# One decoder layer on one core: x loaded twice for its sums of squares, the final scale of a token from three sums per block, and new pacing numbers

## The chip, the cores and the metric

The kernel runs on one core of a Trainium2 chip. The metric is device time in microseconds for the whole program. A core has a matrix engine (TensorE, PE in the profile; its weight loads are PEld), a vector engine (VectorE, DVE), a scalar engine (ScalarE, ACT), a general engine (GpSimd, POOL) and a queue that issues transfers (SyncE, SP). Each runs its own instructions in order and waits on semaphores that others raise.

## The reference

One layer works on 512 tokens of width 2048 in float32. Its input is normed, multiplied by `w_in` and split between an RG-LRU branch and eight pairs of RWKV-7 heads; the two outputs go through `w_o` into the residual. A convolutional GLU follows, then a gated embedding of the token, and a last norm:

```python
u = rmsnorm(h, ln_mix[i]); z = u @ w_cat
...
h = h + jnp.concatenate([out_a, out_b], axis=-1) @ w_o[i]
u = rmsnorm(h, ln_ffn[i])
gate = causal_dwconv(u @ w_gate[i], conv_f_w[i], conv_f_b[i])
h = h + (jax.nn.gelu(gate) * (u @ w_up[i])) @ w_down[i]
u = rmsnorm(h, ln_ple[i])
e = jax.nn.sigmoid(u @ w_ple_gate[i]) * (p[i] @ w_ple_proj[i])
h = h + rmsnorm(e, ln_ple_post[i])
return rmsnorm(h, ln_final)
```

Here `rmsnorm(x, g)` is x * rsqrt(mean(x*x) + eps) * g over the features of a token.

## The kernel before, in words

**Precision.** Nearly every large product is made of three matmuls on values split into a high and a low part (`xh`, `xl` of the activations; `whi`, `wlo` of the weights): high by high, high by low, low by high. ACT makes the high part (`whi`, L123; `xh`, L139), DVE the low part (`wlo`, L124; `xl`, L140). A weight unit is a tile of 128x1024; `wfill` and `wnext` load it on SP into one of two `wraw` buffers, split it, and hand it out.

**Stages.** The *head* (0 to about 60 us) multiplies the 16 tiles of x by the 288 LoRA columns (`lora_z`, L532 to L534: 12 matmuls of 288 columns for an x tile), then begins the RWKV inputs `kt`, `rt`, `vt` of the first head pair (`rwkv_z`, 48 matmuls each). The norm's token scale is applied behind the product, so it is needed only when `kt` is finished. The sum of squares of x runs over partitions: ACT squares an x tile (`square_x`, L508), GpSimd adds it to `lt` (L509, fifteen times), and `tok_rstd` (L182) sums `lt` over partitions with four matmuls of one column. `lora_fin` is called with the number of the dense matmul of `kt`: after the tenth it transposes the LoRA outputs `vk`, `bk`, `kk` (L554, twelve transposes), at the nineteenth it calls `tok_rstd` and `derive`, at the 33rd `rstd_bcast` (L195) spreads the scale over the partitions into `rs`, which `shift` multiplies in.

*Phase 1* (to 867 us) is the token mixing. For each of eight head pairs, `prep` makes the operands, `batch` inverts a triangular matrix per chunk (`Tm`, `Tt`, `Gm`: the products L777 alternate with DVE steps L787, L805), and `chain` walks the state over eight chunks (`us` L858, `st` L879). Between their small matmuls stand dense ones: `w_in`, the LRU gates (L974 to L978) and `w_o`. `merge` writes PE's order from a table of numbers `W`, which says how much time, counted in PE time, is to pass between two steps of a part. The offsets `offp`, `offs`, `offd`, `offl`, `offt` in `W` are priorities: they set in which order the steps of `prep`, of `chain` and `batch`, of the dense products and of the LRU are put on DVE, ACT, GpSimd and SP; `offw` is that of the weight splits. The LRU step of `lru_y` has a scan on DVE (L994) whose input GpSimd makes (L993). At the end of phase 1 a new pool of PSUM tiles begins, and its first users wait for the last readers of the old one.

The *FFN* (to about 2413 us) and its turn to features follow. The *last stage* has four blocks `cb` of 512 output columns, the last of which is done in two halves of 256: per block it makes the projection `pp`, then a gate product `pg` for each of four token tiles `tt`, then `gated` (tanh, L1352), `embed` (DVE L1357 makes e, ACT L1359 sums its squares) and `post` (GpSimd multiplies by the post gain, L1363). The last section, whose order is written out by hand for PE, DVE, ACT and GpSimd, takes the last 256 columns tile by tile: 48 matmuls, tanh, e, the token's scale `rstd` (two small DVE steps L1369, L1370 and a pow on GpSimd L1371), then for the tile before it `residual` (DVE L1377 adds, ACT L1378 squares the finished residual) and `final` (multiply by scale and final gain, L1384, L1385 on ACT and GpSimd or L1387 on DVE, then the DMA out). Tiles named `tmp` have two buffers.

## Time and profile before

| what | value |
|---|---|
| device time, median of 3 runs | 2677.84 us (2676.76 to 2678.28) |
| the profiled execution's own time | 2678.29 us |
| its span in the profile | 2676.5 us |
| mean granted clock of TensorE | 0.994 |
| POOL busy | 282.5 us |
| PE busy from 2600 to 2652.2 us | 52.17 us |
| last PE instruction starts | 2651.89 us |

A row of the timeline gives the start in us, the busy time in us, the engine, the line, the operation, the tile written and the tiles read, the shape, how many instructions are merged, and in brackets the idle time ahead of it and who ended it. Busy times of following matmuls overlap, so their pace is read from the starts. The granted clock is 1.00 when TensorE runs at full speed.

### The profile page before, as it was taken

Reading aid. Unit: us, or ns where it says so; the run is one execution under the profiler, and the core shown is the slowest. Engines: PE = TensorE matmul, PEld = TensorE weight load, DVE = VectorE, ACT = ScalarE, POOL = GpSimd, SP = SyncE. Lnnn points to the kernel's source line nnn. Section 1 sums busy time; section 2 is a strip of 40 time slices with the busy share of each in tenths; the row PEclk is TensorE's granted clock in tenths of the full one; section 3 lists DMA queues with packets and bytes.
Section 4 is the critical chain, followed back from the end, with each engine's and each line's share of the span. In section 5 each row is a group of like instructions: output and inputs, shape, how many; then the busy total and the mean of one; then the engine's idle time right before and its main releaser. Section 6 shows DMA issues by size and latency. Waiting matters only on the chain.

```text
span 2676.5 us, 43392 instructions
## 1 busy us (share of the span) xinstructions
PE 2637.3 (99%) x18440; PEld 2169.2 (81%) x18440; DVE 1682.4 (63%) x2254; ACT 1081.9 (40%) x1520; POOL 282.5 (11%) x219
## 2 busy tenths in 40 slices
PE   9999999999999999999999999999999999999996
PEld 7887787787787888888888888888888888888886
DVE  7664765567564635667666766766666667775235
ACT  5563555547432433333333333333333333334344
POOL 4010100101121300000000000000000000000013
PEclk9999999999999999999999999999999999999998
DMA  5322222222342422332332323223232232332222
GB/s 172 95 76 65 85 76 67 65 84 77 103 134 76 147 87 89 108 100 98 102 103 102 102 95 102 97 100 109 97 110 96 101 107 99 99 110 87 95 88 101
DMA packets 82178, 261.35 MB, mean 98 GB/s; under 512 B 9536, under 2 KB 12224, under 8 KB 81984
## 3 DMA queue, kind: packets, MB, share of 16 engines
q1 hardware_dynamic: 81984, 258.58, 29.3%
q8 instruction: 144, 2.36, 0.4%
q14 instruction: 50, 0.41, 0.1%
...
## 4 chain that ended last, share of the span: by engine, by line
PE 72%; DVE 1%; ACT 0%; POOL 0%; issue 0%; DVEq 0%; POOLq 0%
PE wk L1178 12%; PE wk L1177 12%; PE wk L1176 12%; PE mm L1259 6%; PE mm L1260 6%; PE mm L1258 6%; PE mm L157 2%; PE mm L153 2%; PE mm L155 2%; PE mm L1345 2%; PE mm L1346 2%; PE mm L1347 2%; PE mm L1176 1%; PE mm L1177 1%; PE mm L1178 1%; DVE e L1377 0%
## 5 line engine op out<-in xcount | busy, mean ns | idle before, releaser
L123 ACT ACTIVATE whi<-wraw 128x1024 fp32r<-128x1024 f32 (+2 forms) x363 | 375.3, 1034 | 729.9 <-PE mm L155 173.5
L124 DVE TENSOR_TENSOR wlo<-wraw,whi 128x1024 fp32r<-128x1024 f32 (+2 forms) x363 | 440.6, 1214 | 238.9 <-ACT whi L123 232.9
L1176 PE MATMUL wk<-uh,whi 128*128 128x512 f32 x1408 | 547.8, 389 | 0.0
L1177 PE MATMUL wk<-ul,whi 128*128 128x512 f32 x1408 | 547.7, 389 | 0.0
L1178 PE MATMUL wk<-uh,wlo 128*128 128x512 f32 x1408 | 547.7, 389 | 0.0
L123 ACT ACTIVATE whi<-hw 128x1024 fp32r<-128x1024 f32 x154 | 163.3, 1060 | 464.2 <-PE wk L1177 418.5
L155 PE MATMUL mm<-xl,whi 128*128 128x512 f32 x832 | 332.0, 399 | 1.1 <-DVE xl L140 1.1
L153 PE MATMUL mm<-xh,whi 128*128 128x512 f32 x832 | 330.6, 398 | 1.6 <-DVE y L897 1.6
L157 PE MATMUL mm<-xh,wlo 128*128 128x512 f32 x832 | 330.8, 398 | 0.0
L1177 PEld LDWEIGHTS wk<-ul,whi 128*128 128x128 f32 x1408 | 264.3, 188 | 54.9
L1178 PEld LDWEIGHTS wk<-uh,wlo 128*128 128x128 f32 x1408 | 264.3, 188 | 54.9
L1176 PEld LDWEIGHTS wk<-uh,whi 128*128 128x128 f32 x1408 | 264.3, 188 | 54.8
L124 DVE TENSOR_TENSOR wlo<-hw,whi 128x1024 fp32r<-128x1024 f32 x154 | 188.7, 1225 | 180.8 <-ACT whi L123 178.4
L1259 PE MATMUL mm<-wlo,hid 128*128 128x512 f32 x680 | 265.1, 390 | 0.0
L1258 PE MATMUL mm<-whi,hid 128*128 128x512 f32 x680 | 264.9, 389 | 0.0
L1260 PE MATMUL mm<-whi,hid 128*128 128x512 f32 x680 | 264.8, 389 | 0.0
L1204 POOL TENSOR_TENSOR tmp<-tmp,rsa 128x512 f32<-128x512 f32 x48 | 87.6, 1825 | 1360.8 <-ACT tmp L1203 1360.8
L153 PEld LDWEIGHTS mm<-xh,whi 128*128 128x128 f32 x832 | 156.5, 188 | 36.9 <-issue 5.2
L155 PEld LDWEIGHTS mm<-xl,whi 128*128 128x128 f32 x832 | 156.6, 188 | 36.2 <-issue 2.1
L157 PEld LDWEIGHTS mm<-xh,wlo 128*128 128x128 f32 x832 | 156.5, 188 | 33.5 <-issue 1.9
L1273 DVE TENSOR_TENSOR h<-h,mm 128x512 f32<-128x512 f32 x264 | 175.2, 682 | 0.6
L1258 PEld LDWEIGHTS mm<-whi,hid 128*128 128x128 f32 x680 | 127.6, 188 | 26.4
...
## 6 DMA issues: line engine op xcount, KB each, us to landing
wraw<-wgu SPq DMA_DIRECT2D x192, 512.0 KB, 3.2
...
wraw<-wo SPq DMA_DIRECT2D x20, 256.0 KB, 2.9
tmp<-xT SPq DMA_DIRECT2D x16, 256.0 KB, 2.8
...
```

What stands on the lines that cost most here:

```text
L123: nc.scalar.activation(hi, raw, AF.Copy)
L124: nc.vector.tensor_tensor(lo, raw, hi.bitcast(F32), ALU.subtract)
L153: nc.tensor.matmul(ps, hi[:, k, :], xh, start=first and i == 0, stop=False)
L155: nc.tensor.matmul(ps, hi[:, k, :], xl, start=False, stop=False)
L157: nc.tensor.matmul(ps, lo[:, k, :], xh, start=False, stop=last and i == n - 1)
L1176: TE.matmul(ps, wh[:, k, :], xh, start=h + k == 0, stop=False)
L1177: TE.matmul(ps, wh[:, k, :], xl, start=False, stop=False)
L1178: TE.matmul(ps, wl[:, k, :], xh, start=False, stop=h == 1 and k == 7)
L1258: TE.matmul(ps, x[0][:, k, ts_], w[0][:, k, :], start=first and k == 0, stop=False)
L1259: TE.matmul(ps, x[0][:, k, ts_], w[1][:, k, :], start=False, stop=False)
L1260: TE.matmul(ps, x[1][:, k, ts_], w[0][:, k, :], start=False, stop=last and k == 1)
L1273: V.tensor_tensor(o, o, ps[tt], op)
```

## The change

In the head, x is loaded a second time, by rows of tokens (`xn`, 16 loads of 256 KB into the staging tiles that held `xT`, on SP between the weight loads). ACT squares such a tile and sums along the row in one instruction (`accum_out`, into `ssx`); one reduce, one scaling and a pow give the scale. GpSimd's adds and the four matmuls of `tok_rstd` are gone there. The transposes of the LoRA outputs come after the sixteenth dense matmul of `kt` and use a `ch` tile; the scale is made at the 41st and spread at the 31st of `rt`, and the shift of `kt` follows then. `derive` is cut in two. SP's order in the head is now written by hand with ACT's and DVE's; two more weight tiles of the LoRA are staged and the first two `wz` units are loaded right behind the constants. A third, shorter dummy matmul stands at the start.

In the last stage GpSimd keeps only the pow of single columns. With e' = e * gpost the sum of squares of a token's finished residual is made from three sums: of h*h, of e'*e' (`sg2`, ACT) and of 2*h*e' (`sb`, a DVE multiplication that also sums); `rfin` joins them with the token's scale. So e and h are multiplied by the final gain ahead (`post`, `gain`), `joined` adds them, and `final` only scales (ACT, or DVE for the last block of the last tile).

```diff
@@ the table
-W = dict(... offl=-100, offt=0, pace=790, dpace=1844, late=19660, offs=19710, offd=3000, start=1496, ... rsk=12832, ... t0=5997, tg=1544, tt=1464, lx=4608, lu=1487, ls=1435, ... per=[2, 3, 2, 2, 2, 2, 3, 0], dec7=2111)
+W = dict(... offl=100, offt=-100, pace=381, dpace=1914, late=16634, offs=3000, offd=300, start=1346, ... rsk=8216, ... t0=7550, tg=2186, tt=1559, lx=3928, lu=1429, ls=891, ... per=[2, 3, 2, 2, 3, 1, 3, 0], dec7=2070)
@@ phase1, loads
+        TE.matmul(pz[:, 0:160], z0[:, 0:128], z0[:, 0:160], start=True, stop=True)
...
+        wst = [("gt", 2), ("gt", 2), ("bv", 2), ("bv", 2), ("AR", 2), ("AR", 2), ("MQ", 2), ("NQ", 2), ("MQ", 2), ("NQ", 2)]
...
+        nc.sync.dma_start(self.con1, A["consts"][:, CKEEP:])
+        for i in range(2):
+            wload()
+        self.xn = []
@@ square_x
-            nc.scalar.activation(sq, self.xr[k], AF.Square)
-            nc.gpsimd.tensor_tensor(self.acc, self.acc, sq, ALU.add)
+    def load_xn(self, k):
+        self.xn.append(self.t(self.k1, self.stg[k], bufs=1))
+        self.nc.sync.dma_start(self.xn[k], self.A["xn"][k])
...
+        self.nc.scalar.activation(sq, self.xn[k], AF.Square, accum_out=self.ssx[:, k:k + 1])
@@ lora_z
-        with self.tc.manual_schedule(engines={ET.Activation, ET.DVE}):
+        with self.tc.manual_schedule(engines={ET.Activation, ET.DVE, ET.SP}):
+            self.loads()
...
-                    if k % 4 < 3:
-                        self.square_x(k)
+                    self.load_xn(k)
+                    for _ in range(SQX.get(k, 0)):
...
@@ lora_fin
-        if i == 9:
-            self.zp = [self.mm(), self.aux(), self.t(self.pm, "y", (128, 512), bufs=1)]
+        if i == 15:
+            self.zp = [self.t(self.pm, "ch", (128, 512), bufs=2), self.aux(), self.t(self.pm, "y", (128, 512), bufs=1)]
...
-        if i == 18:
-            self.rl = self.tok_rstd(self.acc, D, RMS_EPS, k1)
+        if i == 40:
+            m = self.pcs[:, NP - 1, 0:4]
+            nc.vector.tensor_reduce(m.unsqueeze(2), self.ssx.rearrange("p (t c) -> p t c", c=4), mybir.AxisListType.X, ALU.add)
+            nc.vector.tensor_scalar(m, m, 1.0 / D, RMS_EPS, ALU.mult, ALU.add)
+            nc.gpsimd.tensor_tensor(m, m, self.mhalf[:, 0:4], ALU.pow)
...
-        if i != 32:
+        if i == 48 + 46:
+            self.derive_lru()
+        if i == 48 + 30:
+            self.rstd_bcast(None, D, RMS_EPS, k1, self.rs, self.rl)
+        if i != 48 + 31:
@@ last stage
-        def post(tt, cb, cs=slice(0, 512)):
-            ee = e[tt * 4 + cb][:, cs]
-            G.tensor_tensor(ee, ee, gpost[cb][:, cs], ALU.mult)
+        def post(tt, cb, cs):
+            n, ix = tt * 4 + cb, slice(tt * 5 + cb, tt * 5 + cb + 1)
+            ee, j1, j2 = e[n][:, cs], T("tmp", 2)[:, cs], T("tmp", 2)[:, cs]
+            V.tensor_tensor(ee, ee, gpost[cb][:, cs], MU)
+            SC.activation(j1, ee, AF.Square, accum_out=sg2[:, ix])
+            V.scalar_tensor_tensor(j2, h3[n][:, cs], 2.0, ee, MU, MU, accum_out=sb[:, ix])
+            V.tensor_tensor(ee, ee, gfin[cb][:, cs], MU)
+        def gain(tt, cb):
+            V.tensor_tensor(h3[tt * 4 + cb], h3[tt * 4 + cb], gfin[cb], MU)
...
+        def rfin(tt, r):
+            t, at, o = T("tl", 6, (128, 1)), slice(tt, tt + 1), slice(tt * 5 + 4, tt * 5 + 5)
+            V.scalar_tensor_tensor(t, sg2[:, o], sge[:, at], r, AD, MU)
+            V.scalar_tensor_tensor(t, sb[:, o], sbe[:, at], t, AD, AD)
+            V.scalar_tensor_tensor(t, t, r, ssh[:, at], MU, AD)
+            V.tensor_scalar(t, t, 1.0 / D, RMS_EPS, MU, ALU.max)
+            return power(t)
...
-                V.scalar_tensor_tensor(e[ix], e[ix], r, h3[ix], ALU.mult, ALU.add)
-                SC.activation(h3[ix], e[ix], AF.Square, accum_out=s2[:, ix:ix + 1])
+                V.scalar_tensor_tensor(e[ix], e[ix], r, h3[ix], MU, AD)
...
-                if cb == 0 or cb == 1 and tt < 3:
-                    SC.activation(e[ix], e[ix], AF.Copy, scale=r)
-                    G.tensor_tensor(e[ix], e[ix], gfin[cb], ALU.mult)
-                else:
-                    V.scalar_tensor_tensor(e[ix], e[ix], r, gfin[cb], ALU.mult, ALU.mult)
+            if act:
+                SC.activation(e[ix], e[ix], AF.Copy, scale=r)
+            else:
+                V.tensor_scalar(e[ix], e[ix], r, None, MU)
```

How the order moves is shown at three places; in such a row stand the line, the operation, the tile written with its number, the tiles read, and the shape.

ACT at the end of the LoRA product, before: the squares (L508) stand ahead of the copies of the LoRA outputs (L540) out of PSUM.

```order
L508 ACTIVATE tmp_100_491<-ktl_152 128x512
L508 ACTIVATE tmp_105_527<-lxl_11_118 128x512
L508 ACTIVATE tmp_106_530<-kt_130 128x512
L123 ACTIVATE whi_542<-wraw_540 128x1024
L508 ACTIVATE tmp_107_533<-ta_142 128x512
L508 ACTIVATE tmp_108_536<-y_29_154 128x512
L540 ACTIVATE vk_519<-wk_176 128x288
L616 ACTIVATE lhi_867<-lraw_862 128x384
L540 ACTIVATE bk_521<-wk_177 128x288
L540 ACTIVATE kk_103_523<-ch_178 128x288
L123 ACTIVATE whi_548<-wraw_546 128x1024
L540 ACTIVATE vk_525<-ch_179 128x288
```

ACT at the same place, after: L525 is the square with its sum, L560 the copy.

```order
L143 ACTIVATE xh_102_483<-y_33_172,par 128x512
L127 ACTIVATE whi_557<-wraw_181 128x1024
L525 ACTIVATE tmp_105_489,pcs<-lx_44_199 128x512
L525 ACTIVATE tmp_106_491,pcs<-lx_49_221 128x512
L560 ACTIVATE vk_532<-wk_115 128x288
L560 ACTIVATE bk_534<-wk_116 128x288
L560 ACTIVATE kk_116_536<-ch_117 128x288
L560 ACTIVATE vk_538<-ch_118 128x288
L525 ACTIVATE tmp_107_493,pcs<-lxh_54_243 128x512
L525 ACTIVATE tmp_108_495,pcs<-lxl_59_265 128x512
L127 ACTIVATE whi_563<-wraw_561 128x1024
L525 ACTIVATE tmp_110_511,pcs<-lxh_64_287 128x512
```

Two squares stand ahead of the first copy now, none between the copies, and nothing that they write is read by GpSimd.

DVE in the batch of the seventh head pair, before: the LRU's last steps (L990 and the scan L994, which the order lists under the same operation name as other three-operand instructions; L995 behind them) beside the batch's second `Gm` (L787), its `Tm` and `Tt` (L805, L806) and the chain's `us` and `st`.

```order
L806 STREAM_TRANSPOSE Tt_7521<-Tm_7520 128x256
L990 SCALAR_TENSOR_TENSOR lxl_1031_7413<-lrc_7542,lxl_1031_7413 128x512
L858 TENSOR_TENSOR us_7746<-ch_7743,NQ_6465 128x64
L994 SCALAR_TENSOR_TENSOR lxl_1029_7404<-lrc_7542,lxl_1031_7413 128x512
L787 TENSOR_TENSOR Gm_7788<-wk_7755,con_157 128x8x16
L995 TENSOR_TENSOR lxl_1029_7404<-lxl_1029_7404,row_172 128x512
L879 SCALAR_TENSOR_TENSOR st_7808<-ch_7748,pcs,so_7809 128x64
L805 TENSOR_TENSOR Tm_7520<-wk_7814,Tm_7520 128x32x4
L806 STREAM_TRANSPOSE Tt_7521<-Tm_7520 128x256
```

DVE in the same batch, after, at its first `Gm` (L822; L805 is the transposition that finishes `Tm`, L452 and L455 a shift, L893 `us`, L1025, L1029 and L1030 the LRU's steps, L128 a weight split):

```order
L804 TENSOR_TENSOR Tt_7625<-Tt_7625,Tm_7624 128x256
L805 STREAM_TRANSPOSE Tm_7624<-Tt_7625 128x256
L452 TENSOR_TENSOR zs<-mm_7535,rs_94 128x512
L1025 SCALAR_TENSOR_TENSOR lxl_1035_7393<-lrc_7500,lxl_1035_7393 128x512
L128 TENSOR_TENSOR wlo_7656<-wraw_7653,whi_7655 128x1024
L455 SCALAR_TENSOR_TENSOR kt_7647<-zs,par,tmp_1082_7649 128x512
L1029 SCALAR_TENSOR_TENSOR lxl_1031_7375<-lrc_7500,lxl_1035_7393 128x512
L1030 TENSOR_TENSOR lxl_1031_7375<-lxl_1031_7375,row_111 128x512
L893 TENSOR_TENSOR us_7680<-ch_7677,NQ_6539 128x64
L822 TENSOR_TENSOR Gm_7722<-wk_7689,con_175 128x8x16
L771 TENSOR_TENSOR NQ_7603<-wk_7724,con_175 128x512
```

The scan stood one row ahead of the second `Gm` and two rows behind L990; now it stands three rows ahead of the first `Gm`, with a split and the end of a shift between it and L1025.

DVE in the last section, before: one whole slot, from the tile's e (L1357) to the four residual additions (L1377).

```order
L1357 SCALAR_TENSOR_TENSOR e_21331<-tmp_22744,hw_3458_22260 128x256
L1369 TENSOR_REDUCE tl_22750<-s_21319 128x1
L1370 TENSOR_SCALAR tl_22750<-tl_22750 128x1
L1369 TENSOR_REDUCE tl_22754<-ss 128x1
L1370 TENSOR_SCALAR tl_22754<-tl_22754 128x1
L1387 SCALAR_TENSOR_TENSOR e_21326<-e_21326,tl_22750,hw_3326_21298 128x512
L1387 SCALAR_TENSOR_TENSOR e_21327<-e_21327,tl_22750,hw_3326_21298 128x512
L1377 SCALAR_TENSOR_TENSOR e_21328<-e_21328,tl_22754,h_8_10608 128x512
L1377 SCALAR_TENSOR_TENSOR e_21329<-e_21329,tl_22754,h_9_10609 128x512
L1377 SCALAR_TENSOR_TENSOR e_21330<-e_21330,tl_22754,h_10_10610 128x512
L1377 SCALAR_TENSOR_TENSOR e_21331<-e_21331,tl_22754,h_11_10611 128x512
```

DVE in the last section, after: the slot of the last tile, from its tanh's first reader (L1507) on; L1444 is `joined`, L1430 and L1435 to L1438 are single columns.

```order
L1507 SCALAR_TENSOR_TENSOR tmp_22961<-tmp_22960,hw_3497_22348 128x256
L1511 SCALAR_TENSOR_TENSOR e_21351<-tmp_22960,hw_3497_22348 128x256
L1444 SCALAR_TENSOR_TENSOR e_21346<-e_21346,tl_22891,h_10_10619 128x512
L1430 TENSOR_SCALAR tl_22970<-ss,se 128x1
L1516 SCALAR_TENSOR_TENSOR tmp_22961,sb<-qz_21328,e_21351 128x256
L1517 TENSOR_TENSOR e_21351<-e_21351,hw_3339_21307 128x256
L1444 SCALAR_TENSOR_TENSOR e_21347<-e_21347,tl_22891,h_11_10620 128x512
L1435 SCALAR_TENSOR_TENSOR tl_22981<-sg_21330,sge,tl_22972 128x1
L1436 SCALAR_TENSOR_TENSOR tl_22981<-sb,sbe,tl_22981 128x1
L1437 SCALAR_TENSOR_TENSOR tl_22981<-tl_22981,tl_22972,ssh 128x1
L1438 TENSOR_SCALAR tl_22981<-tl_22981 128x1
L1444 SCALAR_TENSOR_TENSOR e_21348<-e_21348,tl_22972,h_12_10621 128x512
```

Two multiplications by scale and gain (L1387) and two reduces have left DVE's slot; three operations of 256 columns and four single columns have come in, and the four additions stand between them.

More of the change, by code (lines that the diff above doesn't have):

```diff
@@ L79, in shape_constants @@
     return c
+SQX = {14: 4, 15: 4}
 class Builder:
@@ L253, in phase1, with loads @@
             TE.matmul(pz, z0[:, 0:128], z0, start=True, stop=True)
-        stg = ["lx0", "lx1", "lxh0", "lxl0", "lxh1", "lxl1", "lrc", "kt", "rt", "vt", "Sq", "ta", "kk", "bt", "ktl", "y1"]
-        wst = [("gt", 2), ("gt", 2), ("bv", 2), ("bv", 2), ("AR", 2), ("AR", 2), ("MQ", 2), ("NQ", 2)]
+        TE.matmul(pz[:, 0:160], z0[:, 0:128], z0[:, 0:160], start=True, stop=True)
+        self.scadd = cp.tile([128, NC, C + 1], F32, name="scadd")
+        G.memset(self.scadd, 0.0)
+        G.memset(self.scadd[:, :, 0:1], 1.0)
+        self.TT = cp.tile([128, NC, C], F32, name="TT")
+        G.memset(self.TT, 0.0)
+        self.llo = cp.tile([128, 3, 128], F32R, name="llo")
+        G.memset(self.llo.bitcast(F32), 0.0)
+        self.pcs = cp.tile([128, NP, NC], F32, name="pcs")
+        self.ssx = self.pcs[:, NP - 3:NP - 1].rearrange("p a c -> p (a c)")
+        self.zs = cp.tile([128, S + 1], F32, name="zs")
+        G.memset(self.zs[:, 0:1], 0.0)
+        self.zc = self.t(self.cp, "row", (128, S + 3), bufs=1)
+        G.memset(self.zc[:, 0:3], 0.0)
+        self.zdone = {}
+        self.prepped = {}
+        self.batched = {}
+        with self.tc.manual_schedule(engines={mybir.EngineType.PE}):
+            self.merge(self.dense_stream(self.order))
+    def loads(self):
+        nc, A, k1 = self.nc, self.A, self.k1
+        stg = self.stg = ["lx0", "lx1", "lxh0", "lxl0", "lxh1", "lxl1", "lrc", "kt", "rt", "vt", "Sq", "ta", "kk", "bt", "ktl", "y1"]
+        wst = [("gt", 2), ("gt", 2), ("bv", 2), ("bv", 2), ("AR", 2), ("AR", 2), ("MQ", 2), ("NQ", 2), ("MQ", 2), ("NQ", 2)]
         self.xr, self.wraw = [], []
@@ L541, in lora_z @@
             self.zl.append(z)
-        for k in range(3, KT, 4):
+        for k in range(nsq, KT):
             self.square_x(k)
@@ L591, in rwkv_z, with fin @@
             ps = self.mm()
+            def fin(ps, n, m_, o_):
+                d[n] = self.t(k1, n, bufs=1)
+                self.shift(ps, self.P(m_, j), self.dv(o_, j), d[n])
             for i, _ in enumerate(self.dense(ps, 2, self.xs)):
-                if j == 0 and n == "kt":
-                    self.lora_fin(i)
+                if j == 0 and n != "vt":
+                    self.lora_fin(i if n == "kt" else 48 + i)
+                    if n == "rt" and i == 30:
+                        fin(*first)
                 yield
-            d[n] = self.t(k1, n, bufs=1)
-            self.shift(ps, self.P(m_, j), self.dv(o_, j), d[n])
+            if j == 0 and n == "kt":
+                first = ps, n, m_, o_
+            else:
+                fin(ps, n, m_, o_)
         self.zdone[j] = (d["kt"], d["rt"], d["vt"])
@@ L1332, in phase2 @@
         rsh = k2.tile([128, 4], F32, name="rsh")
+        hq = [T("q" + n, 1, (128, 2, 512)) for n in "xz"]
         ss = k2.tile([128, 20], F32, name="ss")
-        s2 = k2.tile([128, 16], F32, name="s2")
+        sg2, sb = (k2.tile([128, 20], F32, name=n) for n in ("sg2", "sb"))
+        se, sge, sbe, ssh = (k2.tile([128, 4], F32, name=n) for n in ("se", "sge", "sbe", "ssh"))
+        MU, AD = ALU.mult, ALU.add
         e = [self.bp.tile([128, S], F32, tag="x%s%d" % ("hl"[i // 8], 8 + i % 8), name="e%d" % i, bufs=1) for i in range(16)]
@@ new lines, in phase2, with power, early @@
+        AX = mybir.AxisListType.X
+        five = lambda t, tt: t[:, tt * 5:tt * 5 + 5]
+        def power(m):
+            r = T("tl", 6, (128, 1))
+            G.tensor_tensor(r, m, self.mhalf[:, 0:1], ALU.pow)
+            return r
+        def early():
+            V.tensor_reduce(se.unsqueeze(2), ss.rearrange("p (t c) -> p t c", c=5)[:, :, 0:4], AX, AD)
+            V.tensor_scalar(se, se, 1.0 / D, 4 * RMS_EPS, MU, AD)
+            for t, u in ((sg2, sge), (sb, sbe)):
+                V.tensor_reduce(u.unsqueeze(2), t.rearrange("p (t c) -> p t c", c=5)[:, :, 0:4], AX, AD)
+            V.tensor_scalar(ssh, ssh, D * RMS_EPS, None, AD)
```

135 lines of the change are left out of this document (66 added, 69 removed).

## The prediction

> **What bounds the kernel now.** I read the page's first part, then busy time by stage, then who TensorE waits for.
>
> ```profile
> PE 2637.3 (99%) x18440; PEld 2169.2 (81%) x18440; DVE 1682.4 (63%) x2254; ACT 1081.9 (40%) x1520; POOL 282.5 (11%) x219
> ```
>
> PE is busy for all but 39.2 us of the span of 2676.5. No edit changes the number of large matmuls, so that idle time, and the time in which PE counts as busy at a lowered clock, is all there is to win. The profiled execution took 2678.29 us, 1.8 us more than its span and 0.45 us above the median of 2677.84; my sum starts from 2678.3.
>
> ```profile
> 0.00:60.00 60.00, 53.35 (x290) 45.10 (x291) 44.13 (x67) 36.37 (x61) 29.95 (x40) 0.97 0.54 179
> 60.00:867.00 807.00, 798.76 (x10028) 637.99 (x10027) 493.27 (x839) 407.36 (x655) 96.43 (x79) 1.00 0.27 84
> ...
> 2400.00:2600.00 200.00, 200.00 (x911) 164.75 (x911) 77.09 (x84) 77.09 (x126) 13.99 (x10) 1.00 0.28 94
> 2652.20:2676.50 24.30, 0.00 (x0) 0.00 (x0) 17.09 (x22) 9.19 (x24) 11.76 (x11) 0.57 0.37 129
> ```
>
> Columns: stretch, length, busy PE, PEld, DVE, ACT, POOL, granted clock, DMA. PE idles 6.65 us in the head, 8.2 in phase 1, nothing in the 200 us before the last section (nor in the FFN, left out), and 24.3 after the last matmul.
>
> ```profile
> PE mm L974 <- DVE row L964: 2.3, 1, 2.3
> PE mm L554 <- ACT vk L540: 1.9, 1, 1.9
> PE wk L777 <- DVE Gm L787: 1.8, 1, 1.8
> PE mm L153 <- DVE y L897: 1.6, 1, 1.6
> PE wk L534 <- DVE xl L140: 1.5, 3, 0.6
> PE wk L195 <- POOL rsr L186: 1.4, 1, 1.4
> PE mm L155 <- DVE xl L140: 1.1, 1, 1.1
> PE wk L777 <- DVE Tm L770: 1.0, 1, 1.0
> ```
>
> These are PE's waits (total, times, longest). L534, L554 and L195 are the head, the other five phase 1.
>
> **Head.**
>
> ```profile
> 5.45 0.61 PE L532 MATMUL wk<-whi,xh 128*128 128x288 f32 x1 [0.22 <-ACT xh L139]
> 10.25 0.35 PE L532 MATMUL ch<-whi,xh 128*128 128x288 f32 x1
> 34.74 0.30 PE L534 MATMUL wk<-whi,xl 128*128 128x288 f32 x1
> 36.08 0.39 PE L153 MATMUL mm<-xh,whi 128*128 128x512 f32 x1
> 16.60 1.78 DVE L140 SCALAR_TENSOR_TENSOR xl<-lrc,par,xh 128x512 fp32r<-128x512 f32 x1
> 20.07 0.74 DVE L140 SCALAR_TENSOR_TENSOR xl<-kt,par,xh 128x512 fp32r<-128x512 f32 x1
> 36.69 0.63 ACT L508 ACTIVATE tmp<-kt 128x512 f32<-128x512 f32 x1 [2.88 <-POOL lt L509]
> ```
>
> The same split takes 0.74 us alone and 1.78 beside a GpSimd add; that is PE's wait for xl. The change removes all fifteen adds. The 192 LoRA matmuls then run unhindered: 20 at 0.24 us (5.45 to 10.25), 172 at 0.134 (the ten from 34.74 to 36.08), 27.85 in all, ending at 33.5 with the extra dummy matmul ahead (+0.2): **-2.6**. Per x tile PE needs twelve matmuls, 1.6 us; DVE needs one split and half a weight split, about 1.1, so it covers.
>
> ```profile
> 40.42 0.33 PE L554 MATMUL mm<-con,vk 128*128 128x128 f32 x1 [1.89 <-ACT vk L540]
> 43.23 0.78 PE L155 MATMUL mm<-xl,whi 128*128 128x512 f32 x1
> 44.59 0.39 PE L155 MATMUL mm<-xl,whi 128*128 128x512 f32 x1
> 45.98 0.95 PE L182 MATMUL wk<-con,lt 128*128 128x1 f32 x8
> 46.79 0.48 PE L155 MATMUL mm<-xl,whi 128*128 128x512 f32 x1
> tmp<-xT SPq DMA_DIRECT2D x16, 256.0 KB, 2.8
> ```
>
> The transposes waited because ACT's copies stood behind squares, and those behind GpSimd (the 2.88). Ten dense matmuls of 0.23 (six from 44.59 to 45.98) lead from 36.08 to 38.38; from there to 43.23 pass 4.85 us for twelve transposes that need about 1.5: **-3.3**. The three matmuls up to 44.59 took 1.36 instead of 0.69 at the lowered clock: **-0.7**. L182 goes: **-0.8**. The broadcast L195 moves 46 dense matmuls later (10.5 us), so its 1.4 us wait goes: **-1.4**. What is late next is the rstd. The last four row tiles of x stand on SP behind a weight load that waits for a free buffer; I walk them to issue at 44.8, landing at 47.9 (2.8 us for such a load, the last row, and a little for sharing), squares to 49.9, reduce and pow to 52.3, PE at the broadcast at 53.2 (33.5, 79 matmuls of 0.23, 1.5 for the transposes). Cover 0.9 us, so cost nothing. Kt's shift now comes after it and frees kt's PSUM tile about when PE wants it (0 to 1 us). Head **-8.8**, bounds -4 to -11.
>
> **Phase 1.** The paces move work; the counts of dense and small matmuls and of switches between them stay.
>
> ```profile
> 665.72 1.23 DVE L994 TENSOR_TENSOR_SCAN lxl<-lrc,lxl 128x512 f32<-128x512 f32 x1 [1.47 <-POOL lxl L993]
> 666.86 0.27 DVE L787 TENSOR_TENSOR Gm<-wk,con 128x128 f32<-128x128 f32 x1
> 669.00:671.00 2.00, 2.00 (x8) 1.11 (x8) 1.35 (x2) 0.00 (x0) 0.75 (x1) 0.53 0.84 244
> L124 DVE TENSOR_TENSOR wlo<-wraw,whi 128x1024 fp32r<-128x1024 f32 (+2 forms) x363 | 440.6, 1214 | 238.9 <-ACT whi L123 232.9
> 719.30:722.00 2.70, 2.70 (x16) 2.40 (x17) 1.16 (x2) 2.17 (x4) 0.00 (x0) 1.00 0.77 266
> ```
>
> The 1.8 us wait for Gm, in the seventh pair: DVE stood at the LRU scan, which waited for GpSimd, and Gm was behind it. In the new order a weight split and kt's shift fill that wait, and the scan stands ahead of the pair's first Gm instead of its second. From the Tm transpose to that first product PE has 34 dense matmuls (7.8 us; 28 before), and DVE's rows from the transpose to the scan's end are some 5 us. I take the wait as gone; a late input of the scan would bring it back. In the third pair the scan stood ahead of the Tm transpose of the 1.0 us wait, and now stands behind it. For the 2.3 us wait of L974, the transposes that release DVE's backlog come 43 dense matmuls ahead of the gate instead of 21; I leave 0.5 of it. After the two large waits the clock fell to about half (0.53 in the slice quoted, and much the same after the other; with the slices beside it some 1.7 us lost each); after the 1.1 us wait it stayed at 1.00. So -1.8-1.7-1.8-1.7-1.0 = -8.0, and -0.6 at the stage's end, where y L897 is replaced by an hT add some 0.6 us sooner. Against it I set **+3** for new waits of the same kind (two of 1.5 us), since weight splits now go ahead of the chain more often. Phase 1 **-5.6**, bounds -9 to +4.
>
> [...]
>
> **Last stage.**
>
> ```profile
> 2637.69 3.20 DVE L1377 SCALAR_TENSOR_TENSOR e<-e,tl,h 128x512 f32<-128x512 f32 x4 [0.66 <-POOL tl L1371]
> 2644.84 4.81 DVE L1377 SCALAR_TENSOR_TENSOR e<-e,tl,h 128x512 f32<-128x512 f32 x4
> 2650.14 0.43 DVE L1357 SCALAR_TENSOR_TENSOR e<-tmp,hw 128x256 f32<-128x256 f32 x1 [0.49 <-ACT tmp L1352]
> 2650.94 0.15 DVE L1370 TENSOR_SCALAR tl<-tl 128x1 f32<-128x1 f32 x1
> 2649.65 0.46 ACT L1352 ACTIVATE tmp<-mm,rsh 128x256 f32<-128x256 f32 x1
> 2658.30 0.46 ACT L1352 ACTIVATE tmp<-mm,rsh 128x256 f32<-128x256 f32 x1
> 2651.77 0.28 PE L1346 MATMUL mm<-wlo,uh 128*128 128x256 f32 x1
> 2651.89 0.28 PE L1347 MATMUL mm<-whi,ul 128*128 128x256 f32 x1
> 2668.87 3.08 DVE L1387 SCALAR_TENSOR_TENSOR e<-e,tl,hw 128x512 f32<-128x512 f32 x3 [0.72 <-POOL tl L1371]
> ```
>
> A token tile's slot is 8.65 us (tanh to tanh) against PE's 5.76 (48 matmuls 0.12 apart), because DVE's operations take 1.2 us beside GpSimd's instead of 0.7, ACT's squares wait for them, and the next tanh stands behind the squares. New slot on DVE: three STT and one product of 256 columns at 0.43, four joins at 0.66 and five small operations at 0.2, 5.4, with the pow's latency 5.9. The posts of the fourth column block (2.8 us a tile) end some 10 us after the section's first matmul, so the last tile's first STT comes 3.6 us after the last matmul; from there 4.0 to the joins, 2.65 for four of them, 0.45 for the last scaling: 10.7. From the last DVE operation (2671.95) to the span's end are 4.55 us for the DMA out. Tail 15.25 instead of 24.3: **-9.0**, bounds -11 to -5.
>
> In the blocks before, DVE gains 2.8 us per tile and block, over 200 us with 77 busy. Hidden, but for the three block boundaries: two tmp buffers now serve three tiles, so the fourth tile's tanh ends 9.8 to 10.1 us after PE begins the next block, and PE needs its PSUM tile at about 9.9 to 10.1. I take **+0.5** for the three; bounds 0 and 6.
>
> No row of before shows a DVE operation that also sums. Bounds: 0.43 as without, and 0.43 plus 0.27 (the longest small step); I take the first, its nearest row. [...]
>
> **Sum**: 2678.3 - 8.8 - 5.6 - 9.0 + 0.5 = 2655.4; **2655**.
>
> **Rivals.** (1) New waits eat all of phase 1's gain: 2661. For it: a split stands directly or one row ahead of 40 of the chain's 104 DVE steps (29 before). (2) The rstd is late: a weight buffer freed 3 us later stalls PE at the broadcast for 2 us and the clock after it 1.7, and the shift behind it delays PE again: 2659 to 2664. Against it: 0.9 us of cover. [...] (4) Slower: each of those 40 chain steps meets its split just starting. A split is 1.2 us (L124), the step 0.3 (as Gm), handing over 0.3, the cover five matmuls, 1.14: 0.7 us each, 28 in all; 2655 + 6 + 28 = 2689. It passes 2683 only from 0.55 us a step on. Against it: the 29 of before show no wait. (5) The clock opens a window earlier, or phase 1 gains no new wait: 2646 to 2650. That GpSimd still does tile work can be left out: its rows are gone from the order.
>
> **Numbers.** Chances: forecast (2650 to 2660) 0.50, (1) 0.20, (2) 0.08, (3) 0.10, (4) 0.04, (5) 0.08. Two of (1) to (3) together end within 0.2% (5.4 us, about what a measurement of this kernel tells from no change), 0.08 of the above, and 0.01 beyond: faster 0.87, same 0.08, slower 0.05. The range 2646 to 2669 takes in the bounds and leaves out the slower case and the worst sums.
>
> **What would show it.** Right: the first dense matmul near 33.5, no L140 above 0.8 us, PE's waits in the head under 1 us, no wait at Gm, some 15 us after the last matmul. Wrong: a PE wait for the rstd, waits at chain steps, at the blocks' first gates, or a tail above 18.

## The result and the profile after

| what | before | after |
|---|---|---|
| device time, median of 4 runs each, on one chip | 2677.40 us (2676.76 to 2678.28) | 2657.67 us (2656.44 to 2657.95) |
| profiled execution, its own time | 2678.29 us | 2656.44 us |
| its span | 2676.5 us | 2654.6 us |
| first dense matmul of `kt` starts | 36.08 us | 32.01 us |
| first product of phase 1 proper (`wx`) | 85.81 us | 75.23 us |
| first gate product of the FFN | 929.80 us | 916.00 us |
| from the last matmul's end to the span's end | 24.3 us | 15.6 us |

The ratio is 0.9925, with an interval of 0.9908 to 0.9942: 19.7 us less in the medians, 21.9 between the two profiled executions. The forecast was 2655, from 2646 to 2669.

The same starts of TensorE divide the spans: ahead of each stands the same number of large matmuls. The head gave 10.6 us (85.81 to 75.23), phase 1 gave 3.2 (844.0 from `wx` to the FFN, now 840.8), the stretch behind the last matmul 8.7; the boundaries between the blocks of the last stage took back 0.6 (the FFN nothing).

The changed kernel's engines over the span, and busy time by stage (stretch, length, busy PE, PEld, DVE, ACT, POOL, granted clock, DMA):

```profile
PE 2631.0 (99%) x18434; PEld 2164.0 (82%) x18434; DVE 1698.6 (64%) x2356; ACT 1089.4 (41%) x1554; POOL 218.9 (8%) x177
...
60.00:867.00 807.00, 800.44 (x10041) 637.72 (x10040) 510.01 (x876) 409.90 (x665) 95.17 (x81) 1.00 0.28 87
...
2400.00:2600.00 200.00, 200.00 (x933) 165.26 (x932) 98.82 (x137) 88.07 (x157) 1.01 (x1) 1.00 0.28 93
...
2639.00:2654.60 15.60, 0.00 (x0) 0.00 (x0) 9.86 (x25) 7.08 (x14) 2.61 (x4) 0.62 0.52 185
```

PE's idle time fell from 39.2 us to 23.6. DVE is busy 16 us longer, and 22 us longer in the 200 us of the last stage that are quoted (98.82 after 77.09); PE still never stands there. Whom PE waits for, in the whole span (total, times, longest):

```profile
PE wk L769 <- DVE ktl L705: 1.6, 1, 1.6
PE wk L256 <- DVE y L253: 1.5, 1, 1.5
PE ch L891 <- DVE st L914: 0.9, 1, 0.9
PE mm L157 <- DVE hT L447: 0.9, 1, 0.9
PE wk L769 <- DVE y L932: 0.8, 1, 0.8
PE mm L1009 <- ACT lt L1016: 0.5, 1, 0.5
```

L256 is the dummy product at the start. Not one row of the head is left, and neither `Gm` nor the 2.3 us at the LRU gate; what waits now is new, and shorter. Rows of the head:

```profile
7.29 0.41 PE L552 MATMUL ch<-whi,xh 128*128 128x288 f32 x1
7.53 0.30 PE L553 MATMUL ch<-wlo,xh 128*128 128x288 f32 x1
7.66 0.30 PE L554 MATMUL ch<-whi,xl 128*128 128x288 f32 x1
28.08 0.75 DVE L144 SCALAR_TENSOR_TENSOR xl<-y,par,xh 128x512 fp32r<-128x512 f32 x1
32.01 0.39 PE L157 MATMUL mm<-xh,whi 128*128 128x512 f32 x1
50.14 1.04 POOL L579 TENSOR_TENSOR pcs<-pcs,mhalf 128x4 f32<-128x4 f32 x1 [23.69 <-DVE pcs L578]
51.28 1.11 PE L199 MATMUL wk<-con,pcs 128*128 128x128 f32 x8
```

The split takes 0.75 us without GpSimd beside it. The LoRA matmuls come 0.24 us apart up to 7.53 and 0.13 from there: they became faster some 2.8 us sooner than in before. The granted clock reads 1.00 on both sides (4.12 to 7.53 and 7.53 to 10.94) and so doesn't show this change of pace. The pow of the scale ends at 51.18 and PE is at the broadcast at 51.28, so the cover that the forecast put at 0.9 us was hardly there, but it held.

One slot of the last section, DVE first, then ACT:

```profile
2636.88 0.42 DVE L1507 SCALAR_TENSOR_TENSOR tmp<-tmp,hw 128x256 f32<-128x256 f32 x1 [0.89 <-ACT tmp L1506]
...
2638.35 0.42 DVE L1516 SCALAR_TENSOR_TENSOR tmp<-qz,e 128x256 f32<-128x256 f32 x1
2638.69 0.09 DVE L1516 DVE_READ_ACCUMULATOR tmp<-qz,e 128x1 f32 x1
...
2640.73 1.40 DVE L1444 SCALAR_TENSOR_TENSOR e<-e,tl,h 128x512 f32<-128x512 f32 x2
2643.02 0.43 DVE L1507 SCALAR_TENSOR_TENSOR tmp<-tmp,hw 128x256 f32<-128x256 f32 x1 [0.89 <-ACT tmp L1506]
...
2641.91 0.72 ACT L1449 ACTIVATE e<-e,tl 128x512 f32<-128x512 f32 x1 [1.16 <-POOL tl L1417]
2642.53 0.46 ACT L1506 ACTIVATE tmp<-mm,rsh 128x256 f32<-128x256 f32 x1
```

The slot is 6.14 us (2636.88 to 2643.02) instead of 8.65. DVE still stands 0.89 us in each for the tanh L1506, and the last two rows say why: on ACT the tanh stands behind the copy L1449, which waits for GpSimd's pow.

### The profile page after: what moved, and what is told of

Same layout as the page of the kernel before. It is cut to its first block, busy times and chain, and to the rows that moved or that the text cites. A ratio compares the mean times of both kernels' runs of the same rounds, so it can differ in the third digit from the quotient of the medians.

```text
span 2654.6 us, 43517 instructions
## 1 busy us (share of the span) xinstructions
PE 2631.0 (99%) x18434; PEld 2164.0 (82%) x18434; DVE 1698.6 (64%) x2356; ACT 1089.4 (41%) x1554; POOL 218.9 (8%) x177
## 4 chain that ended last, share of the span: by engine, by line
PE 86%; DVE 3%; ACT 2%; issue 1%; POOL 1%; DMA 0%; POOLq 0%; DVEq 0%; ACTq 0%
PE wk L1212 12%; PE wk L1213 12%; PE wk L1211 12%; PE mm L1294 6%; PE mm L1295 6%; PE mm L1293 6%; PE mm L161 5%; PE mm L159 5%; PE mm L157 5%; PE mm L1384 2%; PE mm L1386 2%; PE mm L1385 2%; PE wk L812 1%; PE mm L1211 1%; PE mm L1213 1%
## 5 line engine op out<-in xcount | busy, mean ns | idle before, releaser
L127 ACT ACTIVATE whi<-wraw 128x1024 fp32r<-128x1024 f32 (+1 forms) x361 | 373.9, 1036 | 707.3 <-PE mm L159 173.5
L128 DVE TENSOR_TENSOR wlo<-wraw,whi 128x1024 fp32r<-128x1024 f32 (+1 forms) x361 | 440.7, 1221 | 210.6 <-ACT whi L127 205.6
L128 DVE TENSOR_TENSOR wlo<-hw,whi 128x1024 fp32r<-128x1024 f32 x154 | 188.7, 1225 | 181.1 <-ACT whi L127 178.6
```

Of the source, the lines that this page charges most:

```text
L127: nc.scalar.activation(hi, raw, AF.Copy)
L128: nc.vector.tensor_tensor(lo, raw, hi.bitcast(F32), ALU.subtract)
```

## The experiments

Twelve runs were made in three groups, each group on one chip together with before, whose medians there were 2676.43, 2677.53 and 2678.47. Where a run was timed only once, its time is that of the profiled execution. The change itself was measured beside other executions of before, so a single run is compared with it by stretches of the profile more than by its time.

**The old pacing numbers in the changed kernel.** Only the table `W` is that of before.

```diff
-W = dict(... pace=381, dpace=1914, late=16634, offs=3000, offd=300, ... dec7=2070)
+W = dict(... pace=790, dpace=1844, late=19660, offs=19710, offd=3000, ... dec7=2111)
```

> The changed kernel with the table W of before, nothing else. Theory A (the paces are worth phase 1's gain and nothing else): head and last stage as in the changed kernel (first product with wx near 75.2 us, tail 15.6), but from there to the first FFN matmul 844.0 us again instead of 840.8, with waits for row L999 or Gm near 2 us and the clock falling behind them; about 2661 us. Rival B (the new head suits only the new table): the first product with wx comes later than 76 us and phase 1 takes over 846 us; 2664 us or more. Rival C (phase 1 gains from the new head, not from the table): 840.8 us, 2657.7 us.

Measured: 2659.61, span 2657.8, 3.2 more than after. All of it lies between `wx` and the FFN (844.3 us, theory A's number), and the old waits are back:

```profile
PE mm L1009 <- DVE row L999: 2.2, 1, 2.2
PE wk L812 <- DVE Gm L822: 2.2, 2, 1.8
PE mm L157 <- DVE y L932: 1.6, 1, 1.6
```

So the waits belong to the table. What phase 1 gained by losing them is taken up again below, because this one pair of executions misleads.

**Two dummy matmuls instead of three.**

```diff
-        TE.matmul(pz[:, 0:160], z0[:, 0:128], z0[:, 0:160], start=True, stop=True)
```

> The changed kernel without the third, shorter dummy matmul. Theory A (it closes PE's gap of 0.22 us behind the dummies, and the clock opens a window earlier for it): the LoRA's matmuls stay 0.24 us apart until about 10.2 us as before, and the first dense matmul comes at 34 to 35 us instead of 32.0; 2659.5 to 2660.5 us. Rival B (where the clock opens is chance): it opens near 7.3 us here too, the first dense matmul comes at 31.8, and the time is that of the changed kernel, 2657.5 us.

Measured: 2656.90 (4 runs, ratio 0.9928, 0.9912 to 0.9945). The LoRA's matmuls became faster at about 7 us again, as rival B has it. The third dummy isn't what made that early.

**GpSimd's fifteen additions put back into the head**, on a tile that nobody reads.

```diff
+                        nc.gpsimd.tensor_tensor(pa, pa, self.xs[k][0].bitcast(F32), ALU.add)
```

> The changed kernel with fifteen GpSimd additions of 128x512 put back into the head, behind the splits of x, on a tile that nothing reads. Theory A (they slow DVE, and so the splits that PE waits for): splits of x near 1.8 us where an addition runs, PE waits for xl of 1 to 3 us in all, first dense matmul at 33.5 to 35 us instead of 32.0. Rival B (what held the head was only ACT's queue behind squares that waited for GpSimd): the splits get slower, but PE does not wait, 32.0 us; in both, the transposes and the broadcast stay without a wait.

Measured: 2666.05, span 2664.3, 9.6 more than after; the first dense matmul starts at 38.92, far behind theory A's 33.5 to 35, and `wx` at 83.7. PE's waits in the head:

```profile
PE wk L558 <- DVE xl L144: 5.4, 6, 1.6
PE wk L199 <- POOL pcs L583: 1.3, 1, 1.3
```

A split beside an addition, and the pow of the scale, in the timeline:

```profile
12.10 1.78 DVE L144 SCALAR_TENSOR_TENSOR xl<-lxl,par,xh 128x512 fp32r<-128x512 f32 x1
...
58.55 1.04 POOL L583 TENSOR_TENSOR pcs<-pcs,mhalf 128x4 f32<-128x4 f32 x1 [17.99 <-DVE pcs L582]
```

The split takes 1.78 us again, and the head is 8.4 us longer than in after. Ahead of the first dense matmul the additions cost 6.9 us, more than the 4.1 that the change gained there; so the run shows that GpSimd beside DVE makes PE wait, and is not before's head over again. Behind that matmul they cost 1.5 of the 6.5 us gained. The second wait was not expected. It isn't GpSimd's other work, for GpSimd had stood idle for 17.99 us when the pow began: the last four row tiles of x were issued from 49.78 us on instead of 42.57, behind a weight load, and their squares came late. That is the late scale of the prediction's rival (2), at 1.3 us.

**GpSimd's tile work put back beside the last section**, two products of 128x512 a slot, unread.

```diff
+                    for _ in range(2):
+                        G.tensor_tensor(pd, pd, gfin[0], MU)
```

> The changed kernel with two GpSimd multiplications of 128x512 per token tile in the last section, on a tile that nothing reads. Theory A (GpSimd's work itself made DVE's slot long): the joins next to them take 1.2 instead of 0.7 us, a slot takes 8 us instead of 6.14, and the tail is 20 to 24 us instead of 15.6; 2662 to 2666 us. Rival B (the chain over the squares of the finished residual made the slot long, GpSimd was beside it): slot and tail grow by less than 1.5 us in all, 2657.5 to 2659.5 us. GpSimd's pow stands behind the multiplications too; if that alone delays, the joins stay at 0.7 us and the slot grows.

Measured: 2663.25; the stretch behind the last matmul is 20.3 us instead of 15.6. DVE and GpSimd in one slot:

```profile
2640.74 1.49 DVE L1513 SCALAR_TENSOR_TENSOR e<-tmp,hw 128x256 f32<-128x256 f32 x1
...
2639.09 2.85 POOL L1527 TENSOR_TENSOR ld<-ld,hw 128x512 f32<-128x512 f32 x2
```

DVE's e takes 1.49 us instead of 0.42 while GpSimd is at it, and the slot 7.33 instead of 6.14. That is theory A, but not on the joins, which stay at 0.7 us each; e alone makes up nearly all of the slot's growth. It is 4.7 of the 8.7 us, and not the old slot.

**The other way round: before, with GpSimd's tile work of the last stage on DVE.** The squares and the way a scale is made stay as they were.

```diff
-            G.tensor_tensor(ee, ee, gpost[cb][:, cs], ALU.mult)
+            V.tensor_tensor(ee, ee, gpost[cb][:, cs], ALU.mult)
...
-                if cb == 0 or cb == 1 and tt < 3:
-                    SC.activation(e[ix], e[ix], AF.Copy, scale=r)
-                    G.tensor_tensor(e[ix], e[ix], gfin[cb], ALU.mult)
-                else:
-                    V.scalar_tensor_tensor(e[ix], e[ix], r, gfin[cb], ALU.mult, ALU.mult)
+                V.scalar_tensor_tensor(e[ix], e[ix], r, gfin[cb], ALU.mult, ALU.mult)
```

> The kernel before, with GpSimd's tile work of the last stage (the multiplications by the post gain and by the final gain) put on VectorE, and the squares of the finished residual, ScalarE's part and the way a token's scale is made left as they were; nothing is left out. Theory A (GpSimd beside VectorE, and the queue behind it, was what made a token tile's slot long): the slot falls from 8.65 us to about 7, the stretch after the last matmul from 24.3 to about 19, the time by about 5 us to 2672. Theory B (the chain from the residual over ScalarE's squares to the next tanh made it long, and only the three sums per block take that away): the slot stays at 8 us or more, the stretch after the last matmul at 22 or more, and the time within 2 us of before.

Measured: 2669.89. ACT's tanh of two slots, and the four additions on DVE:

```profile
2644.59 0.45 ACT L1352 ACTIVATE tmp<-mm,rsh 128x256 f32<-128x256 f32 x1
...
2652.08 0.46 ACT L1352 ACTIVATE tmp<-mm,rsh 128x256 f32<-128x256 f32 x1
...
2649.35 2.73 DVE L1377 SCALAR_TENSOR_TENSOR e<-e,tl,h 128x512 f32<-128x512 f32 x4
```

The additions take 2.73 us instead of 4.8, the slot 7.49 instead of 8.65, and the stretch behind the last matmul is 19.7 instead of 24.3. So of the last section's 8.7 us, taking GpSimd off makes 4.6. The other 4.1 are left for the scale from three sums and the order that goes with it, which no run has by itself. The remaining 3.8 us of this run's gain are no work of the edit: they lie in the head (1.3) and in phase 1 (2.6).

**The new table in before.**

```diff
-W = dict(... pace=790, dpace=1844, late=19660, offs=19710, offd=3000, ... dec7=2111)
+W = dict(... pace=381, dpace=1914, late=16634, offs=3000, offd=300, ... dec7=2070)
```

> The kernel before with the table of numbers of the changed kernel; nothing else is changed. Theory A (the gain of phase 1 is the table's alone): the stretch from the first product of phase 1 to the first matmul of the feed-forward stage shortens from 844.0 us to about 840.8, the waits of 1.8 to 2.3 us at Gm and at the LRU gate are gone, and the time is about 2674. Theory B (the table fits only the changed order of the head, which hands over other tiles at other times): new waits of over 1 us take their place, and the time stays at 2677 or goes up.

Measured: 2675.20. The stretch from `wx` to the FFN is 1.8 us shorter than in before, and its waits there are those of after, none longer than 1.6. Theory A by its waits; why the gain is shorter than 3.2 us is the next question.

**Holds of TensorE, to see when the clock falls.** At eight steps of the FFN ACT runs a chain of copies into the tile of the next gate product.

```diff
+HOLD = {14: 5, 17: 6, 21: 7, 25: 8, 29: 9, 33: 10, 37: 12, 41: 14}
...
+                    for _ in range(HOLD[f]):
+                        SC.activation(s, s, AF.Copy)
```

> The changed kernel with eight holds of TensorE in the feed-forward stage: at eight of its steps ScalarE runs a chain of 5, 6, 7, 8, 9, 10, 12 and 14 copies into the tile that the next gate product writes, behind a small extra product; nothing else is changed. TensorE has about 2.7 us of other products to do meanwhile and so should stand for some 0.5 to 5.5 us, each hold longer than the one before. Theory A (as the waits of the kernel before read: no loss at 1.1 us, loss at 1.8): the granted clock stays at 1.00 behind holds under about 1.7 us and falls to about half for some 3 us behind every longer one, each of which costs some 1.7 us beside the wait itself. [...] Theory C (what decides is a count over a fixed window and not the length of the hold): holds of like length differ.

Measured: 2696.71. The holds did not grow as meant: ACT's weight splits stood behind the chain, so the first hold was a wait of 1.3 us and one of 0.8 close together, and each of the other seven one of 1.3 and one of 0.5, the last three followed some 4 us later by one of 1.2 to 1.6. That told more. The granted clock fell (to 0.50) behind four of the seven equal pairs, and not behind the other three. Every fall lasted 3.41 us, and the falls of this execution begin at 189.68, 1329.73, 1555.01, 1684.71, 1814.42, 2203.54 and 2210.36 us (read from slices of 0.1 us): 334, 66, 38, 38, 114 and 2 times 3.4133 apart, each within 0.01 us. In this execution the clock is thus set anew at the edges of a fixed grid. Busy time between such edges (busy PE is the second number, the clock the last but two):

```profile
1944.13:1947.54 3.41, 1.78 (x8) 1.24 (x7) 1.88 (x3) 2.98 (x5) 0.31 (x1) 1.00 0.37 137
1947.54:1950.95 3.41, 3.41 (x17) 2.78 (x16) 0.72 (x1) 0.00 (x0) 0.22 (x1) 1.00 0.48 153
2206.95:2210.36 3.41, 1.74 (x7) 0.85 (x6) 1.91 (x2) 2.91 (x5) 0.00 (x0) 1.00 0.01 1
2210.36:2213.78 3.42, 3.42 (x10) 2.65 (x9) 0.00 (x0) 0.84 (x2) 0.00 (x0) 0.50 0.77 229
```

A stretch with 1.74 us of work is followed by one at half clock, a stretch with 1.78 is not. In this stage of this execution, where all products are large, the border lies between 1.63 and 1.67 us of idle time in a stretch. Theory C, then: not the length of a wait decides, but how much of it falls between two edges. Theory A is out.

**The changed kernel once more**, unchanged, to test this.

> The changed kernel once more, unchanged, beside the next three on one chip. What it tells apart is whether the lowered clock behind phase 1's wait of 1.61 us at L769 is settled by the kernel or by the execution. Theory A (the execution: the clock is set anew at the edges of a grid of 3.413 us that starts anywhere, for the next stretch by how much TensorE idled in the last): the profile shows the wait at the same distance from the first products, and the clock falls behind it only where the greater part of the wait, over some 1.5 us, lies between two edges; the edges can be read from the moment at which the first matmuls become faster. Theory B (the length of the wait): no fall, as in the first profile of this kernel. Time 2655 to 2659 under both.

Measured: 2656.76 (4 runs, 2656.20 to 2657.76; ratio 0.9921, 0.9908 to 0.9935). The wait at L769 is 1.61 us as in the first profile of the changed kernel, with no fall behind it. The first matmuls show no clear change of pace here, but every profile has a fall behind its last matmul (before's begins at 2655.7, that of the first profile of after at 2642.6), and this one's begins at 2643.26: 719 and 718 stretches earlier stand edges at 189.07 and 192.48. The first cuts the wait; the stretch ahead of it holds 1.12 us of idle time, the one behind it 0.53. The edges of the first profile follow from the 7.53 at which its matmuls became faster, 53 stretches earlier:

```profile
185.02:188.43 3.41, 2.95 (x88) 2.17 (x86) 3.38 (x6) 0.63 (x1) 0.80 (x1) 1.00 0.32 71
188.43:191.84 3.41, 2.20 (x21) 1.88 (x22) 2.50 (x4) 2.27 (x4) 2.25 (x3) 1.00 0.42 165
```

And the kernel of the tanh experiment below, with the same wait, its edges from its fall:

```profile
187.17:190.59 3.42, 1.74 (x84) 1.51 (x80) 3.05 (x5) 1.45 (x3) 2.93 (x2) 1.00 0.64 230
190.59:194.00 3.41, 3.41 (x12) 2.60 (x9) 2.55 (x4) 3.01 (x6) 0.11 (x2) 0.50 0.08 16
```

The same wait, cut by an edge into 0.46 and 1.21 us of idle time, or 1.12 and 0.53, and once whole (1.68): no fall, twice, and a fall. Of ten profiles with this wait, seven show a fall behind it and three (both of after, and the one with two dummies) don't. Theory A is what this bears out, on both profiles of after. Its "over some 1.5 us" is no sharp border, though. The stretch with this wait with two dummies, and with GpSimd in the last section:

```profile
187.84:191.25 3.41, 1.86 (x20) 1.58 (x21) 2.50 (x4) 1.95 (x3) 2.59 (x3) 1.00 0.50 184
...
186.01:189.42 3.41, 1.93 (x83) 1.34 (x81) 3.38 (x6) 0.63 (x1) 1.81 (x2) 1.00 0.57 190
```

The first, with 1.55 us of idle time, is followed by no fall, the second, with 1.48, by one. A fall came after 1.40 (GpSimd in the head) and 1.50 (before, at `Gm`) as well, and none after 1.68 at the gate in the next run. So over all stages the border lies between 1.4 and 1.7 us, and idle time alone doesn't place it. The stretches that fell at 1.50 or less hold 68 to 83 products, most of them small; how such products count is open.

**The old table in the changed kernel, timed.** The edit is that of the first experiment.

> The changed kernel with the pacing numbers of before, a second time, now timed. Theory A (the new paces are worth what the waits of TensorE were shortened by, and the first two profiles of this pair differed by the chance of the clock besides): 0.5 to 2 us slower than the changed kernel on the same chip in the median, and the waits at Gm (1.8 us) and at the LRU gate (2.2 us) stand in the profile, with or without a fall of the clock behind each. Theory B (the waits and the clock behind them always go together): 3 us or more slower.

Measured: 2660.32 (5 runs, 2658.59 to 2660.88; ratio 0.9932, 0.9920 to 0.9944), 3.6 above the kernel of the run before on the same chip. By its number that is theory B, and theory A's 0.5 to 2 us is missed; by the profile it isn't B, for the wait at the gate (2.2) stands here without a fall and the one at `Gm` with one. The table's worth is read from like executions: from `wx` to the FFN, counted to a fixed later matmul, the new table's stretch is 936.5, 936.7 and 937.1 us where no fall comes, the old one's 937.3 in the one profile without a fall (before with DVE in the last stage). With one fall they are 937.8 to 939.2 and 939.0 to 940.1, and the profile of before, with two, has 939.9. So without falls the table is worth 0.2 to 0.8 us, by that one profile. The rest of the 3.6 would have to be fewer falls, and that is not shown: from `wx` to the FFN the four profiles of the old table have 2, 1, 1 and 0, ten of the new one have one in seven and none in three. How many the unprofiled executions had can't be seen.

**Tanh ahead of the first scaling in the last section.**

```diff
-                        final(tt - 1, rf, 0)
...
+                    if tt:
+                        final(tt - 1, rf, 0)
```

> The changed kernel with one row moved in the last section: on ScalarE the tanh of a token tile stands ahead of the copy that scales the first block of the tile before it; nothing is left out. Theory A (the slot of 6.14 us is set by the tanh that stands behind that copy, which waits for GpSimd's pow): the slots fall to between 5.76, TensorE's own 48 matmuls, and 5.9, the wait of 0.89 us at the first VectorE step of a slot goes, and the stretch after the last matmul shrinks by 0.7 to 1.5 us: about 2656.5, ratio to the kernel before 0.9920. Theory B (VectorE's own work and the pow's way set the slot): slot 6.1 or more, the time within 0.4 us of the changed kernel, or longer, since the scaled block and its transfer come later.

Measured: 2655.08 (5 runs, ratio 0.9915, 0.9901 to 0.9928). DVE no longer waits for the tanh, and the stretch behind the last matmul is 12.8 us instead of 15.6, twice the most that was expected: the slots of the last tiles follow DVE's own 5.2 us, below PE's 5.76, and make up for the start. ACT and DVE in one slot:

```profile
2641.57 0.47 ACT L1505 ACTIVATE tmp<-mm,rsh 128x256 f32<-128x256 f32 x1 [0.26 <-PE mm L1386]
2642.48 0.72 ACT L1449 ACTIVATE e<-e,tl 128x512 f32<-128x512 f32 x1 [0.43 <-POOL tl L1417]
...
2637.44 0.42 DVE L1508 SCALAR_TENSOR_TENSOR tmp<-tmp,hw 128x256 f32<-128x256 f32 x1
...
2642.62 0.42 DVE L1508 SCALAR_TENSOR_TENSOR tmp<-tmp,hw 128x256 f32<-128x256 f32 x1
```

**The same, beside the changed kernel on one chip.**

> The changed kernel with tanh ahead of the first scaling on ScalarE in the last section, a second time, beside the changed kernel. Theory A (the shorter last section is the whole of the difference): median 2 to 3.5 us below the changed kernel, and the stretch after the last matmul again some 2.9 us shorter. Theory B (the first pair differed by chance): within 1 us of the changed kernel.

Measured: 2655.69 (5 runs, 2653.78 to 2656.05; ratio 0.9913, 0.9900 to 0.9927). The stretch is again 2.9 us shorter (12.7). The median is only 1.1 below the changed kernel's, between the two theories; its profile had the fall behind L769 and the other's had none. The fastest executions of both, 2653.78 and 2656.20, are 2.4 apart.

**Two more kinds of GpSimd work on DVE, in phase 1**, on top of this.

```diff
-        G.tensor_tensor(rt, rt, kt, ALU.mult)
+        V.tensor_tensor(rt, rt, kt, ALU.mult)
...
-                G.tensor_tensor(self.rsa, self.rsa, rc, ALU.add)
+                V.tensor_tensor(self.rsa, self.rsa, rc, ALU.add)
```

> The kernel of the run before, with two more kinds of GpSimd tile work put on VectorE: the product of rt and kt (eight of 128x512) and the running sum of squares of the LRU output. Nothing is left out. In the changed kernel these two run beside the VectorE step that TensorE waits for at 189 us and stretch it from 0.67 us to 1.64. Theory A (the two engines hold each other up there as in the head): that step takes 0.7 us, the wait shrinks from 1.61 to about 0.6, no clock falls behind it, and the time is 1 to 2.5 us below the kernel of the run before. Theory B (VectorE gets some 16 us more to do in phase 1 and passes it on): new waits elsewhere in phase 1, the time the same or up to 3 us more.

Measured: 2654.13 (4 runs, 2652.16 to 2654.55; ratio 0.9909, 0.9896 to 0.9923), 1.6 below the kernel of the run before: the lowest median of all, though the executions of the two overlap. Their profiles, each with one fall, differ by 1.9 us from `wx` to the FFN. The time is theory A's and its reason is wrong. The step that PE waits for, in the changed kernel:

```profile
187.85 1.64 DVE L705 TENSOR_TENSOR ktl<-kt,th 128x512 f32<-128x512 f32 x1
```

And here, with one of the two new rows ahead of it:

```profile
188.31 0.68 DVE L718 TENSOR_TENSOR rt<-rt,kt 128x512 f32<-128x512 f32 x1
188.91 0.68 DVE L705 TENSOR_TENSOR ktl<-kt,th 128x512 f32<-128x512 f32 x1
```

The step is down from 1.64 to 0.68 us, but the two that came to DVE stand ahead of it, and it ends at 189.6 rather than 189.5: the wait stays (1.7), and the clock fell behind it. What went are the waits of 0.9 and 0.8 at L891 and at L769 for y. In the changed kernel the 0.9 came from a scan and a weight split ahead of the chain's step; here that step comes ahead of both.

## Why the prediction was right, and where not

The forecast of 2655 was 2.7 us below the median and 1.4 below the profiled execution. The mechanisms were those named, in all three places, but the sizes differ, and that the sum came so near is in part luck: the head gave 1.8 more than forecast and phase 1 2.4 less.

**Head: -8.8 forecast, -10.6 measured.** The gain before the first dense matmul was 4.1 instead of 2.6, behind it 6.5 instead of 6.2. That GpSimd beside DVE held up the first part is borne out by the additions put back, which cost 6.9 us there. In the second part they cost only 1.5; that its gain comes from the moved transposes and broadcast is read from the waits that are gone (1.9 at L554, 1.4 at L195) and from the fall at 41 us that is gone, and no run shows it by itself. The term that was mis-sized is the first: the sum kept before's 20 matmuls at 0.24 us. That number is set by the grid: before's falls at 457.50 and 669.12, counted back, put an edge at 10.35, where its matmuls do become faster, and three further profiles with a fall agree in the same way (6.69, 6.67 and 6.90). Two other executions of the old head reached `wx` at 84.5; against them the head's gain is 9.3.

**The rstd** was on time by 0.1 us instead of 0.9. PE came to it 1.9 us sooner than forecast, and the squares ended sooner too. Rival (2) was close.

**Phase 1: -5.6 forecast, -3.2 measured.** The waits at `Gm`, `Tm` and L974 went and the stage's end came sooner, as said. Of the sum, 2.2 us were waits (5.2 of old ones gone, 3 of new ones come) and 3.4 the clock. From `wx` to the FFN PE's idle time fell by 1.7 us, from 8.2 to 6.5. The clock's part was 2.9: before is busy for 835.75 us there, and 832.87 in the run of before's order that kept both waits and had neither fall (DVE in the last stage). So the prediction counted as a part of the two waits what is a chance of each execution. The third term was put at nothing: PE is busy for 834.24 us there in the changed kernel, 1.4 more than in that run, with the same 10190 products. Together that makes -1.7 - 2.9 + 1.4 = -3.2.

Where the 1.4 us come from is open. One group of rows looks like the cause: four of the eight `bonus` products (L726) are now followed at once by a product of the chain instead of a dense one. The changed kernel:

```profile
756.18 1.02 PE L726 MATMUL wk<-rt,bdr 128*128 128x512 f32 x2
757.13 0.33 PE L891 MATMUL ch<-st,MQ 64*64 64x64 f32 x4
```

And before, where the same product is L691:

```profile
492.88 1.12 PE L691 MATMUL wk<-rt,bdr 128*128 128x512 f32 x2
493.44 0.79 PE L157 MATMUL mm<-xh,wlo 128*128 128x512 f32 x1
```

Two such halves take 0.95 us ahead of a small product and 0.56 ahead of a dense one. But in before the dense product behind them takes longer in its turn (0.79 against the usual 0.39). Counted over the same 87 products around these rows, the two orders take the same time, first after, then before:

```profile
755.95:758.97 3.02, 3.02 (x87) 2.03 (x86) 1.80 (x4) 0.46 (x1) 0.00 (x0) 1.00 0.56 194
...
491.30:494.31 3.01, 3.01 (x87) 2.04 (x86) 2.49 (x6) 1.42 (x2) 0.00 (x0) 1.00 0.03 5
```

And the counts of switches between large and small products do stay, as the prediction had it: 160 each way in both kernels, from `wx` to the FFN, with products of 512 columns as the large ones. Rival (1) took part of the gain, not all. The 0.3 us for handing over in rival (4) was an estimate, and no run shows it: in before `Gm` ends on DVE at 667.13 and PE's product of it starts at 667.18.

**The clock's rule.** The prediction took the length of a wait for what decides. The runs show a grid of 3.413 us and a border somewhat below half a stretch of idle time, between 1.4 and 1.7 us: a wait of 1.6 us may cost a fall or nothing, and a fall is 1.7 us more by an estimate from its 3.41 us at half clock. The earlier window of rival (5) came: such a stretch is 3.413 us, and the matmuls of the head became faster at 7.53 instead of 10.35.

**Last stage: -9.0 forecast, -8.7 measured**, the slot 6.14 instead of 5.9, because the tanh still stood behind a copy that waits for the pow. The block boundaries took 0.6 instead of 0.5. The four joins, put at 0.66 us each, take 0.68 (2.73 for the four of the last tile, from 2646.87). A scalar_tensor_tensor (STT) that also sums is busy for some 0.09 us more than a plain one (0.42 and 0.09 in the slot above), and the next step starts 0.55 us behind its start instead of 0.35 (L1517 behind L1516, L1511 behind L1507). Rival (3), to which the chances give 0.10, was a dearer STT with a sum; no run shows it dearer than by that.
